# A two-layer diffusion step on one core: splits of 16 weight units on VectorE, the scan's work ahead of the q and k units, x to memory from SyncE, and later statistics

## The chip, the cores and the metric

The kernel runs on one NeuronCore of a Trainium2 chip. The time is the device time of one execution in microseconds, measured on the chip; three executions of the kernel before took 1505.66 to 1508.61 us, with a median of 1507.27.

## What is computed

Two layers of a hybrid backbone act on 640 tokens (128 of a prompt, 512 latent ones) with 1024 features, all in fp32. Every sub-layer is a norm, a modulation with shift and scale, a mixer, and a gated addition to x:

```python
hs = modulate(rmsnorm(xs, norm1_g[layer]), shift, scale)
if layer % 2 == 0:                       # pooling | gated convolution
    ys = even_mixer(hs, ab_w_in, pool_w, pool_scale, conv_w, ab_w_out)
else:                                    # attention | S5
    q_s, k_s, v_s, u_s = jnp.split(hs @ cd_w_in, 4, axis=-1)
    o_s = from_heads(neighbourhood_attention(to_heads(q_s), to_heads(k_s), to_heads(v_s), ...))
    d_s, _, _ = s5_bidirectional(u_s, state_s5_re, state_s5_im, *ssm_args)
    ys = jnp.concatenate([o_s, d_s], axis=-1) @ cd_w_out
xs = xs + gate1 * ys
hs = modulate(rmsnorm(xs, norm2_g[layer]), shift2, scale2)
xs = xs + gate2 * (jnp.square(jax.nn.relu(hs @ mlp_w1)) @ mlp_w2)
```

The prompt goes through the same layers, with plain attention instead of the windowed one. `s5_bidirectional` projects u to complex states, runs a linear recurrence over time in both directions, projects back, and multiplies with a gate (GLU).

## The kernel before

Features lie on the partitions: x is 8 row blocks of 128 features by 640 tokens. An fp32 product is made of three fp32r matmuls: a weight is split into wh (rounded) and wl (the rest), an activation into hh and hl (or dh and dl), and wl·hh, wh·hh and wh·hl are summed in PSUM.

Weights stream as 178 units of 512 KB, in the order of use: 0 to 15 and 16 to 23 the mixer of layer 0, 24 to 87 its MLP, 88 to 91 u of layer 1, 92 and 93 q0 and k0, 94 to 97 v, 98 to 103 q and k of the pairs of heads 1 to 3, 104 and 105 the GLU, 106 to 113 the output projection, 114 to 177 the second MLP. Of each unit SyncE's queue (SP) loads `raw`, ScalarE (ACT) rounds it to wh (L263), and wl is the difference, made by GpSimd (POOL, L270) or, for the units in the set ON_VECTOR, by VectorE (DVE, L268). The VectorE ones are put off: `defer` keeps them in a list until `flush`, which runs ahead of an evacuation, when TensorE comes to that unit, or when its buffer is needed again. At most four units are split at a time; `retire` frees one and splits the next.

Each engine has one queue, and works through it in the order in which the program is written; buffers and data are guarded by semaphores. The places that matter:

- A norm lies between the last four blocks of x (`out_units`, by halves of 320 tokens) and the first two units of the next layer (`in_units`). While TensorE makes the second half, VectorE does for each block the gated addition to x (L446), ACT its square (L388), and GpSimd, the last time VectorE, adds up the squares (acc, L389). Between them stand the modulated rows of the first half: t (VectorE, L431), hh (ACT, L434), hl (VectorE, L440). In `in_units` TensorE goes through k = 0 to 7 with two units at a time, first on half 0 (p = 0 and 1). `stats_half(1)` is written after the row k = 4 of p = 0: matmuls of acc (L395), a division, a square root on ACT (L399) and four small steps on VectorE (L398 to L403); `spread` (L412) after the first row of p = 1 lays the result over the partitions, and the rows of half 1 follow.
- Such a point comes three times in the part that the change touches: ahead of the MLP of layer 0 (units 24 on), ahead of u of layer 1 (units 88 on), and ahead of the second MLP (units 114 on).
- Ahead of u of layer 1, four DMAs on ACT's queue bring x to memory (`xst`, L1084), since its two buffers are used again (tags xa and xb: q and k, and the outputs of attention).
- At the end of the first MLP GpSimd also makes tables for S5 (`s5_build`, bd, s5f, s5g, L963 to L983) which TensorE transposes (L996).
- The S5 input (`s5_in`, blocks b = 0 to 15 with their tables et(b), L1228) is interleaved with the rows of the units of q0 and k0: `mid` lists pairs of row and block.
- The scan over S (`s5_scan`) runs on VectorE: first local sums (`add`, L1254 to L1257), then steps of width one, then copies, then eight fix-ups q = 0 to 7 (L1288, L1290). It is a generator; `scan_pump(n)` issues the next n pieces.
- Attention has 20 steps (`attention`, `step`) of softmax (L1386, L1388), exponentials on ACT, transposes and products; they stand behind the units of q and k by the table ATT (2, 3, 2, 3, 2, 3), the rest at the end. Within the steps a piece of the scan is pumped, `s5_turn` transposes S (copies L1472), and `s5_out(f)` (L1489, L1491) stands behind the steps of S5_OUT.

Of the kernel before, what the change touches and what calls it, by code (L numbers as in the profile page):

```python
# [7 lines left out]
F32R = mybir.dt.float32r  # L8
# [5 lines left out]
T = 640  # L14
TP = 128
EPS = 1e-6
KC = 8
# [158 lines left out]

ON_VECTOR = {*range(16, 24), *range(40, 80), *range(104, 106)}

N_EARLY = 88

# [1 line left out]

ATT = (2, 3, 2, 3, 2, 3)

S5_OUT = (9, 16, 18, 19)


class Rows:  # L190
# [12 lines left out]
class Net:  # L203
# [289 lines left out]
    def in_units(self, u0, rhs, evac, nxt, ahead=True):  # L493
        for h in range(2):
            for p in range(2):
                pt = self.ps()
                us = (u0 + 2 * p, u0 + 2 * p + 1)
                for k in range(KC):
                    for i, u in enumerate(us):
                        self.mms([(pt[:, i, :320], HALVES[h])], u, rhs[k], 128 * k, k == 0, k == KC - 1)  # L500
                    if h == 0 and p == 0 and k == 4:
                        self.stats_half(1)
                    if h == 0 and p == 1 and k == 0:
                        self.spread()
                        nxt(1, range(KC))
                self.flush()
                evac(h, p, pt)
                if h == 1:
                    for u in us:
                        self.retire(u, p == 0 or ahead)  # L510
# [551 lines left out]
    def layer1(self, u0, nxt_in, nxt_out):  # L1062
        nc, one, tc, A = self.nc, self.one, self.tc, self.A
# [12 lines left out]
        uf = one.tile([128, 4, 8, 80], F32, name="uf", tag="va")  # L1076
# [3 lines left out]
        self.scr = [dl[:, a:a + 640] for a in (3712, 4352)]  # L1080
        self.S = one.tile([128, 32, 2, 90], F32, name="S", tag="dh")
        self.load()
        for f in range(0, KC, 2):
            nc.scalar.dma_start(self.xst[:, f:f + 2], self.x.pair(f))  # L1084
        self.in_units(u0, self.hs, lambda h, p, pt: self.u_out(uf, h, p, pt), nxt_in, False)

        xq = one.tile([128, 4, T], F32, name="xq", tag="xa")
        self.q, self.k = (xq[:, 0], xq[:, 2]), (xq[:, 1], xq[:, 3])
        o = one.tile([128, 4, T], F32R, name="o0", tag="xb")
        self.os = [(o[:, 0], o[:, 1]), (o[:, 2], o[:, 3])]  # L1090
        att = self.attention()
        next(att)

        def qk(j, s, mid=()):
            u = u0 + 4 + 2 * j + s + (4 if j else 0)
            pt = self.ps()
            for k in range(KC):
                for b in (b for a, b in mid if a == k):
                    self.s5_in(b)
                self.mms(self.both(pt), u, self.hs[k], 128 * k, k == 0, k == KC - 1)  # L1100
            self.flush()
            o = (self.q, self.k)[s][j % 2]
            nc.scalar.activation(o.rearrange("p (a b) -> p a b", a=2), pt[:, :, :320], AF.Copy, scale=0.125 if s == 0 else 1.0)
            self.bias_ahead()
            self.turn(u)
            if s:
                nc.sync.dma_start(A["nk"][:, j], o[:, 0:128])

        qk(0, 0, [(4 + b, b) for b in range(4)])
        qk(0, 1, [(2 * (b - 4) // 3, b) for b in range(4, 16)])  # L1110
        self.scan = self.s5_scan()
        self.at = [one.tile([128, 8, 128], F32, name="at0"), None]
        nc.sync.dma_start(self.at[0], self.ast[:, 0:8])
        o = one.tile([128, 2, T], F32R, name="o1")
        self.os.append((o[:, 0], o[:, 1]))
        self.v_units(u0 + 6)
        self.step_no, self.yf = 0, None

        def step():
            next(att)  # L1120
            i = self.step_no
            self.step_no += 1
            self.scan_pump(1)
            if 8 <= i < 12:
                self.s5_turn(2 * i - 16)
                self.s5_turn(2 * i - 15)
            if i in S5_OUT:
                self.s5_out(S5_OUT.index(i))

        next(att)  # L1130
        for j in range(1, 4):
            for s in range(2):
                qk(j, s)
                for _ in range(ATT[2 * j - 2 + s]):
                    step()
            if j == 1:
                for q in range(2):
                    self.ft_load(q)
        o = one.tile([128, 2, T], F32R, name="o2", tag="la")
# [98 lines left out]
    def s5_scan(self):  # L1238

        S, v = self.S, self.nc.vector
        Z = S.rearrange("p n m c -> p (n m) c")
        sh = lambda w: [128, 32, 2, w]
        c = self.carry.rearrange("p (i n m k) -> p i n m k", i=2, n=32, m=2)
        rows = lambda i: c[:, i].rearrange("p n m k -> p (n m) k")
        v.memset(S[:, :, :, 0:10], 0.0)
        v.tensor_copy(S[:, :, 0, 2], self.s5sc[:, 3])
        v.tensor_scalar(S[:, :, 1, 2], self.s5sc[:, 4], -1.0, None, op0=OP.mult)
        yield  # L1250

        def add(cur, prv, j, w):
            t1, t2 = (t[:, :64 * w].rearrange("p (n m k) -> p n m k", n=32, m=2) for t in self.scr)
            v.tensor_mul(t1, self.apr[:, :, :, j:j + 1].to_broadcast(sh(w)), prv)  # L1254
            v.tensor_mul(t2, self.api[:, :, :, j:j + 1].to_broadcast(sh(w)), prv[:, :, ::-1])
            v.tensor_add(cur, cur, t1)
            v.tensor_add(cur, cur, t2)  # L1257

        add(S[:, :, :, 12:13], S[:, :, :, 2:3], 0, 1)
        yield  # L1260
        for j in range(1, 8):
            add(S[:, :, :, 10 * j + 10:10 * j + 20], S[:, :, :, 10 * j:10 * j + 10], 0, 10)
            yield

        add(S[:, :, :, 81:84:2], S[:, :, :, 80:83:2], 7, 2)
        f = self.one.tile([128, 2, 32], F32, name="fin")
        v.tensor_copy(f[:, 0], S[:, :, 0, 81])
        v.tensor_scalar(f[:, 1], S[:, :, 1, 81], -1.0, None, op0=OP.mult)
        self.nc.sync.dma_start(self.A["st"], f)
        yield  # L1270
        for k in range(4, 9):
            add(S[:, :, :, 80 + k:81 + k], S[:, :, :, 79 + k:80 + k], 7, 1)
            yield

        v.tensor_copy(Z[:, :, 1], Z[:, :, 80])
        v.tensor_copy(Z[:, :, 3:10], Z[:, :, 82:89])
        v.tensor_copy(rows(0), Z[:, :, 1:10])
        v.memset(rows(0)[:, :, 1:2], 0.0)
        v.tensor_copy(c[:, 1], c[:, 0, :, ::-1])
        yield  # L1280
        w = [128, 8, 7, 9]
        for q in range(8):
            n = slice(8 * q, 8 * q + 8)
            cur = Z[:, n, 10:80].rearrange("p a (j k) -> p a j k", k=10)[:, :, :, 1:10]
            ts = [t[:, :504].rearrange("p (a j k) -> p a j k", a=8, j=7) for t in self.scr]
            for i, (t, a) in enumerate(zip(ts, (self.apr, self.api))):
                a = a.rearrange("p n m j -> p (n m) j")[:, n, 0:7]
                v.tensor_mul(t, a[:, :, :, None].to_broadcast(w), rows(i)[:, n][:, :, None].to_broadcast(w))  # L1288
            for t in ts:
                v.tensor_add(cur, cur, t)  # L1290
            if q % 2:
                yield

    def v_units(self, u0):
        nc = self.nc
# [285 lines left out]
```

## Time and profile before

| | us |
|---|---|
| median of 3 runs | 1507.27 |
| the profiled execution | 1508.45 |
| its span | 1506.4 |
| TensorE busy | 1441.6 |
| VectorE busy | 883.3 |
| GpSimd busy | 623.8 |
| ACT busy | 483.9 |

The mean granted clock of TensorE over the span was 0.976 of full speed. A timeline row gives the start in us from the span's start, the duration, the engine, the line, what is written from what, and, in brackets, for how long the engine was idle before and what ended that. TensorE is busy nearly throughout; the short idle stretches and the stretches at a lower clock are what remains. A wait is read in two steps: which instruction of TensorE waits, and what its releaser in turn was waiting for.

### The profile page before, as it was taken

The numbers are of one execution on the slowest core, as the hardware profiler recorded it, in microseconds if no ns is written. First come the engines' busy times: TensorE is split into PE (matmuls) and PEld (weight loads), VectorE is DVE, ScalarE is ACT, GpSimd is POOL, SyncE is SP. The second block draws the span as 40 slices with busy tenths as digits, with TensorE's granted clock in tenths as the row PEclk, the third lists the DMA queues.
The fourth block names the chain that finished last, engine by engine and source line by source line (L and its number), as shares of the span: only waits on it lengthen the run. The fifth ranks groups of instructions, "written<-read, shape, count | busy, mean of one in ns | idle before, by whom it ended". The sixth has DMA issues, their size and how long they took to land.

```text
span 1506.4 us, 24126 instructions
## 1 busy us (share of the span) xinstructions
PE 1441.6 (96%) x9757; PEld 1409.8 (94%) x9757; DVE 883.3 (59%) x1602; ACT 483.9 (32%) x856; POOL 623.8 (41%) x445
## 2 busy tenths in 40 slices
PE   7999999999999999899899979999999999999997
PEld 7999899999999999899888878999999999999997
DVE  7899975899898888824429575336561221221223
ACT  4321234313323422333332435534421321321321
POOL 2333032327797778645324312053333333333342
PEclk9999999999999999999889979999999999999999
DMA  9245531514554445434762312621342222222211
GB/s 378 83 169 180 185 125 57 170 57 168 194 173 164 174 164 174 140 96 138 260 195 91 97 49 95 219 84 56 119 148 70 82 72 70 84 72 70 84 57 70
DMA packets 73966, 193.30 MB, mean 128 GB/s; under 512 B 15360, under 2 KB 23936, under 8 KB 73344
## 3 DMA queue, kind: packets, MB, share of 16 engines
q1 hardware_dynamic: 68400, 186.37, 36.5%
q10 hardware_dynamic: 5456, 5.40, 1.1%
q8 instruction: 77, 1.26, 0.4%
q14 instruction: 33, 0.27, 0.1%
HBM read 170.51 MB, written 22.54 MB: 128 GB/s over the span
## 4 chain that ended last, share of the span: by engine, by line
PE 70%; DVE 14%; issue 6%; POOL 3%; ACT 3%; DMA 2%; ACTq 0%; DVEq 0%; SPq 0%; POOLq 0%
PE pp L301 62%; DVE condb L332 3%; DVE hl L440 1%; PE bk L1424 1%; PE pp L1491 1%; PE pp L1306 1%; POOL wl L270 1%; PE bk L1228 1%; DVE x L446 1%; DMA raw<-wts 1%; ACT wh L263 1%; POOL s5q L964 1%; PE pp L1406 1%; DVE wl L268 1%; PE bk L996 1%
## 5 line engine op out<-in xcount | busy, mean ns | idle before, releaser
L270 POOL TENSOR_TENSOR wl<-raw,wh 128x1024 fp32r<-128x1024 f32 x128 | 316.4, 2476 | 617.9 <-ACT wh L263 613.9
L301 PE MATMUL pp<-hh,wl 128*128 128x320 f32 x1472 | 363.4, 318 | 2.3 <-POOL wl L270 1.2
L301 PE MATMUL pp<-hl,wh 128*128 128x320 f32 x1472 | 356.9, 313 | 7.1 <-DVE hl L440 5.1
L301 PE MATMUL pp<-hh,wh 128*128 128x320 f32 x1472 | 356.5, 313 | 0.0
L263 ACT ACTIVATE wh<-raw 128x1024 fp32r<-128x1024 f32 x178 | 186.2, 1051 | 321.1 <-PE pp L301 228.8
L301 PE MATMUL pp<-dh,wl 128*128 128x320 f32 x1152 | 280.1, 310 | 5.5 <-DVE x L446 2.7
L301 PE MATMUL pp<-dl,wh 128*128 128x320 f32 x1152 | 277.9, 309 | 0.0
L301 PE MATMUL pp<-dh,wh 128*128 128x320 f32 x1152 | 277.9, 309 | 0.0
L301 PEld LDWEIGHTS pp<-hl,wh 128*128 128x128 f32 x1472 | 254.6, 191 | 9.2 <-DVE hl L440 6.3
L301 PEld LDWEIGHTS pp<-hh,wl 128*128 128x128 f32 x1472 | 254.7, 192 | 5.5 <-issue 2.6
L301 PEld LDWEIGHTS pp<-hh,wh 128*128 128x128 f32 x1472 | 255.6, 192 | 0.0
L446 DVE SCALAR_TENSOR_TENSOR x<-pp,mod,x 128x128 f32<-128x128 f32 (+2 forms) x240 | 91.4, 432 | 242.7 <-PE pp L301 242.4
L301 PEld LDWEIGHTS pp<-dh,wl 128*128 128x128 f32 x1152 | 195.9, 188 | 8.8 <-issue 5.5
L301 PEld LDWEIGHTS pp<-dl,wh 128*128 128x128 f32 x1152 | 196.5, 188 | 0.3 <-DVE dl L451 0.3
L301 PEld LDWEIGHTS pp<-dh,wh 128*128 128x128 f32 x1152 | 196.5, 188 | 0.0
L332 DVE SCALAR_TENSOR_TENSOR condb<-ada,condb 128x1024 bf16<-128x1024 f32 x124 | 184.6, 1489 | 2.3
L772 DVE SCALAR_TENSOR_TENSOR pp<-pp,t 128x640 f32<-128x640 f32 x64 | 53.1, 830 | 190.2 <-ACT t L771 190.2
L771 ACT ACTIVATE t<-pp 128x640 f32<-128x640 f32 x64 | 45.1, 704 | 259.0 <-PE pp L301 243.2
L389 POOL TENSOR_TENSOR acc<-acc,sq 128x320 f32<-128x320 f32 (+1 forms) x36 | 40.0, 1112 | 117.1 <-ACT sq L388 112.5
L268 DVE TENSOR_TENSOR wl<-raw,wh 128x1024 fp32r<-128x1024 f32 x50 | 69.3, 1387 | 0.0
L388 ACT ACTIVATE sq<-x 128x320 f32<-128x320 f32 (+1 forms) x51 | 29.0, 570 | 117.2 <-DVE x L446 110.9
L774 DVE TENSOR_TENSOR dl<-pp,dh 128x640 fp32r<-128x640 f32 x64 | 52.6, 821 | 3.6
(249 smaller groups left out, 1633.2 us busy)
## 6 DMA issues: line engine op xcount, KB each, us to landing
raw<-wts SPq DMA_DIRECT2D x178, 512.0 KB, 3.5
ada<-ada SPq DMA_DIRECT2D x80, 512.0 KB, 4.5
spare<-ada SPq DMA_DIRECT2D x16, 512.0 KB, 3.6
est<-s5e SPq DMA_DIRECT2D x16, 256.0 KB, 5.0
fst<-s5fc SPq DMA_DIRECT2D x16, 256.0 KB, 2.0
et<-est SPq DMA_DIRECT2D x16, 256.0 KB, 3.7
ft<-fst SPq DMA_DIRECT2D x8, 512.0 KB, 4.1
x<-x SPq DMA_DIRECT2D x8, 320.0 KB, 5.4
```

The source lines that it names most:

```text
L263: self.nc.scalar.activation(wh, raw, AF.Copy)
L268: self.defer(lambda: self.nc.vector.tensor_sub(wl, raw, wh.bitcast(F32)))
L270: self.nc.gpsimd.tensor_sub(wl, raw, wh.bitcast(F32))
L301: self.nc.tensor.matmul(o, a[:, w], b[:, s], start=first and n == 0, stop=last and n == 2)
L332: self.nc.vector.scalar_tensor_tensor(self.junk, a, 1.0, self.condb[:, c], op0=OP.mult, op1=OP.mult, accum_out=self.mod[:, l, j, f, c:c + 1])
L388: self.nc.scalar.activation(q, self.x[f][:, s], AF.Square)
L389: (self.nc.vector if f >= last else self.nc.gpsimd).tensor_add(self.acc[:, s], self.acc[:, s], q)
L440: self.nc.vector.scalar_tensor_tensor(o, t, b, h.bitcast(F32), op0=OP.add, op1=OP.subtract)
L446: self.nc.vector.scalar_tensor_tensor(self.x[f][:, s], p[:, s.start - 320 * h:s.stop - 320 * h], self.mod[:, l, j, f, c:c + 1], self.x[f][ ...
L771: self.nc.scalar.activation(t, p, AF.Relu)
L772: self.nc.vector.scalar_tensor_tensor(p, p, 0.0, t, op0=OP.max, op1=OP.mult)
L774: self.defer(lambda: self.nc.vector.tensor_sub(dl, p, dh.bitcast(F32)))
```

## The change

- ON_VECTOR gets 16 units more: 24 to 27, 80 to 83, 88 to 91 and 114 to 117. VectorE makes their wl, GpSimd no longer.
- `stats_half(1)` is written two rows later, after k = 6.
- The four DMAs of x to memory leave ACT's queue. SP issues two after the evacuation of half 0, p = 1, and two after the unit of k0. The tile o0, which uses the second buffer of x again, is made after the units of v.
- The blocks of the S5 input stand one row later with q0 (5, 6, 7, 7) and two to a row from row 1 on with k0.
- The scan is no longer pumped in the steps but ahead of the six units of q and k, in portions of ATT_SCAN; a fix-up is a piece of its own. S is turned after the steps 6, 9, 11 and 13, and the first part of the S5 output stands behind step 8.

```diff
-ON_VECTOR = {*range(16, 24), *range(40, 80), *range(104, 106)}
+ON_VECTOR = {*range(16, 28), *range(40, 84), *range(88, 92), *range(104, 106), *range(114, 118)}
-S5_OUT = (9, 16, 18, 19)
+S5_OUT = (8, 16, 18, 19)
+
+S5_TURN = (6, 9, 11, 13)
+ATT_SCAN = (5, 3, 2, 2, 2, 1)
...
-                    if h == 0 and p == 0 and k == 4:
+                    if h == 0 and p == 0 and k == 6:
                         self.stats_half(1)
...
-        for f in range(0, KC, 2):
-            nc.scalar.dma_start(self.xst[:, f:f + 2], self.x.pair(f))
-        self.in_units(u0, self.hs, lambda h, p, pt: self.u_out(uf, h, p, pt), nxt_in, False)
+
+        def keep_x(f):
+            for f in (f, f + 2):
+                nc.sync.dma_start(self.xst[:, f:f + 2], self.x.pair(f))
+
+        def evac(h, p, pt):
+            self.u_out(uf, h, p, pt)
+            if h == 0 and p == 1:
+                keep_x(0)
+
+        self.in_units(u0, self.hs, evac, nxt_in, False)
...
-        qk(0, 0, [(4 + b, b) for b in range(4)])
-        qk(0, 1, [(2 * (b - 4) // 3, b) for b in range(4, 16)])
+        qk(0, 0, [(min(5 + b, 7), b) for b in range(4)])
+        qk(0, 1, [(1 + (b - 4) // 2, b) for b in range(4, 16)])
+        keep_x(4)
...
-            self.scan_pump(1)
-            if 8 <= i < 12:
-                self.s5_turn(2 * i - 16)
-                self.s5_turn(2 * i - 15)
+            if i in S5_TURN:
+                f = S5_TURN.index(i)
+                self.s5_turn(2 * f)
+                self.s5_turn(2 * f + 1)
...
             for s in range(2):
+                self.scan_pump(ATT_SCAN[2 * j - 2 + s])
                 qk(j, s)
...
-            if q % 2:
-                yield
+            yield
```

On VectorE, in the last round of the second norm (ahead of u of layer 1), before:

```order
L440 SCALAR_TENSOR_TENSOR hl<-t,mod,hh 128x192
L446 SCALAR_TENSOR_TENSOR x<-pp,mod,x 128x320
L389 TENSOR_TENSOR acc<-acc,sq 128x320
L431 SCALAR_TENSOR_TENSOR t<-x,gs,bk 128x128
L431 SCALAR_TENSOR_TENSOR t<-x,gs,bk 128x192
```

and after the change (the lines have moved by three):

```order
L443 SCALAR_TENSOR_TENSOR hl<-t,mod,hh 128x192
L271 TENSOR_TENSOR wl<-raw,wh 128x1024
L449 SCALAR_TENSOR_TENSOR x<-pp,mod,x 128x320
L392 TENSOR_TENSOR acc<-acc,sq 128x320
L434 SCALAR_TENSOR_TENSOR t<-x,gs,bk 128x128
```

A split stands between the low parts of one round and the x of the next; the same holds for the rounds before it and for the other two norms. The fourth split stands behind the last hl here, and behind the steps of the statistics in the first and the third norm.

On SP, from u of layer 1 to the unit of k0 (up is u in the scan's layout, uds its copy in memory, rpb a bias table, et the tables of S5), before:

```order
L1212 DMA et<-est 128x512 x4
L252 DMA raw<-wts 128x1024
L1206 DMA up<-uds 128x8x80 x2
L252 DMA raw<-wts 128x1024 x2
L1206 DMA up<-uds 128x8x80 x2
L252 DMA raw<-wts 128x1024
L1331 DMA attc<-rpb 64x1x265 x4
L1212 DMA et<-est 128x512 x4
```

and after:

```order
L1226 DMA et<-est 128x512 x4
L255 DMA raw<-wts 128x1024
L1089 DMA xst<-x 128x1280 x2
L1220 DMA up<-uds 128x8x80 x2
L255 DMA raw<-wts 128x1024 x2
L1220 DMA up<-uds 128x8x80 x2
L255 DMA raw<-wts 128x1024
L1344 DMA attc<-rpb 64x1x265 x4
L1226 DMA et<-est 128x512 x4
```

Two of the four transfers of x now stand ahead of the first loads of up; the other two stand further on, behind the unit of k0.

On VectorE in attention, where the second pair of fix-ups is done (L1288 and L1290 are one fix-up, L1472 the copies of the turn, L1386 and L1388 the softmax), before:

```order
L451 TENSOR_TENSOR o_7555<-pp,o_7555 128x128
L1288 TENSOR_TENSOR up<-apr,up 128x504
L1288 TENSOR_TENSOR up<-api,up 128x504
L1290 TENSOR_TENSOR S<-S,up 128x8x7x9 x2
L1288 TENSOR_TENSOR up<-apr,up 128x504
L1288 TENSOR_TENSOR up<-api,up 128x504
L1290 TENSOR_TENSOR S<-S,up 128x8x7x9 x2
L1472 COPY S<-tn 64x8x80 x2
L1386 TENSOR_TENSOR pp<-pp,bm 128x2x256
L1388 TENSOR_REDUCE sm<-pp 128x2
```

and after, ahead of the unit of k in which they are now issued, with the end of the step before it:

```order
L454 TENSOR_TENSOR o_8031<-pp,o_8031 128x128
L1485 COPY S<-tn 64x8x80 x2
L1302 TENSOR_TENSOR up<-apr,up 128x504
L1302 TENSOR_TENSOR up<-api,up 128x504
L1304 TENSOR_TENSOR S<-S,up 128x8x7x9 x2
L1302 TENSOR_TENSOR up<-apr,up 128x504
L1302 TENSOR_TENSOR up<-api,up 128x504
L1304 TENSOR_TENSOR S<-S,up 128x8x7x9 x2
L271 TENSOR_TENSOR wl<-raw,wh 128x1024
L1401 TENSOR_REDUCE sm<-pp 128x2
```

Before, the next step's softmax follows two fix-ups and the copies; now two fix-ups stand once in front of a whole unit, and a split of the GLU's weights after them.

## Rows read from the trace of the kernel before

**Rows 1.** Stretches: length, busy us (count) by engine, granted clock, DMA share, GB/s.
```profile
208.00:240.00 32.00, 29.10 (x181) 28.55 (x180) 23.46 (x55) 14.29 (x31) 12.18 (x7) 0.89 0.21 66
605.00:640.00 35.00, 30.13 (x202) 28.81 (x200) 29.90 (x41) 13.22 (x26) 25.62 (x25) 0.95 0.41 138
699.00:737.00 38.00, 31.77 (x178) 30.57 (x178) 28.48 (x61) 16.14 (x37) 18.99 (x13) 0.82 0.55 187
752.00:790.00 38.00, 34.34 (x230) 33.88 (x229) 8.87 (x32) 11.94 (x22) 11.68 (x8) 0.87 0.67 199
819.00:937.00 118.00, 105.74 (x758) 98.43 (x755) 75.28 (x159) 55.55 (x153) 34.70 (x34) 0.91 0.29 87
1022.00:1050.00 28.00, 25.11 (x154) 24.57 (x154) 20.63 (x49) 12.85 (x28) 12.17 (x7) 0.88 0.23 75
```

**Rows 2.** Waits of TensorE in the first norm: total us, times, longest.
```profile
PE pp L301 <- DVE hl L440: 1.6, 1, 1.6
PE bk L395 <- DVE acc L389: 1.3, 1, 1.3
```

**Rows 3.** Waits of TensorE from the second norm to k0.
```profile
PE bk L412 <- DVE st L403: 3.1, 1, 3.1
PE bk L1228 <- ACT S L1233: 2.0, 1, 2.0
```

**Rows 4.** Waits of TensorE in the last units of the first MLP.
```profile
PE bk L996 <- POOL s5f L965: 4.9, 2, 3.6
```

**Rows 5.** Waits of TensorE in attention.
```profile
PE pp L1432 <- DVE o L451: 5.8, 2, 4.4
PE pp L1491 <- DVE S L1472: 3.3, 1, 3.3
```

**Rows 6.** Timeline of VectorE in the second norm: start, duration, instruction, idle before.
```profile
705.79 0.54 DVE L446 SCALAR_TENSOR_TENSOR x<-pp,mod,x 128x320 f32<-128x320 f32 x1
706.25 1.24 DVE L431 SCALAR_TENSOR_TENSOR t<-x,gs,bk 128x128 f32<-128x128 f32 x4
708.16 3.22 DVE L440 SCALAR_TENSOR_TENSOR hl<-t,mod,hh 128x128 fp32r<-128x128 f32 x4 [0.67 <-ACT hh L434]
711.31 0.54 DVE L446 SCALAR_TENSOR_TENSOR x<-pp,mod,x 128x320 f32<-128x320 f32 x1
```

**Rows 7.** Timeline of GpSimd in the same round.
```profile
707.92 2.40 POOL L270 TENSOR_TENSOR wl<-raw,wh 128x1024 fp32r<-128x1024 f32 x1
```

**Rows 8.** Timeline of VectorE in attention.
```profile
888.22 0.68 DVE L1288 TENSOR_TENSOR up<-api,up 128x504 f32<-128x504 f32 x1
888.81 1.40 DVE L1290 TENSOR_TENSOR S<-S,up 128x504 f32<-128x504 f32 x2
...
899.27 1.23 DVE L268 TENSOR_TENSOR wl<-raw,wh 128x1024 fp32r<-128x1024 f32 x1
```

**Rows 9.** Timeline of TensorE at full clock, pairs of matmuls in k0's unit.
```profile
753.71 0.46 PE L301 MATMUL pp<-hh,wh 128*128 128x320 f32 x2
754.01 0.45 PE L301 MATMUL pp<-hl,wh 128*128 128x320 f32 x2
```

**Rows 10.** Timeline of GpSimd at the end of the first MLP.
```profile
625.80 2.46 POOL L270 TENSOR_TENSOR wl<-raw,wh 128x1024 fp32r<-128x1024 f32 x1 [8.69 <-ACT wh L263]
...
631.20 0.79 POOL L965 TENSOR_TENSOR s5f<-s5f,s5q 128x288 f32<-128x288 f32 x1
...
634.37 1.65 POOL L965 TENSOR_TENSOR s5f<-s5f,s5q 128x288 f32<-128x288 f32 x1
```

**Rows 11.** Timeline of ACT and its queue behind the second norm.
```profile
720.00 8.06 ACTq L1084 DMA_DIRECT2D xst<-x  x3
728.12 0.21 ACT L399 ACTIVATE st<-st 128x3 f32<-128x3 f32 x1 [7.97 <-DMA ast<-a]
```

**Rows 12.** Timeline of VectorE in the scan's local sums.
```profile
819.40 0.82 DVE L1256 TENSOR_TENSOR S<-S,up 128x640 f32<-128x640 f32 x1
820.25 2.92 DVE L1257 TENSOR_TENSOR S<-S,up 128x640 f32<-128x640 f32 x1
```

More of the change, by code (lines that the diff above doesn't have):

```diff
@@ L1082, in layer1 @@
         self.load()
-        for f in range(0, KC, 2):
-            nc.scalar.dma_start(self.xst[:, f:f + 2], self.x.pair(f))
-        self.in_units(u0, self.hs, lambda h, p, pt: self.u_out(uf, h, p, pt), nxt_in, False)
+        def keep_x(f):
[6 more added lines that the diff above has]
+        self.in_units(u0, self.hs, evac, nxt_in, False)
         xq = one.tile([128, 4, T], F32, name="xq", tag="xa")
         self.q, self.k = (xq[:, 0], xq[:, 2]), (xq[:, 1], xq[:, 3])
-        o = one.tile([128, 4, T], F32R, name="o0", tag="xb")
-        self.os = [(o[:, 0], o[:, 1]), (o[:, 2], o[:, 3])]
+        self.os = []
         att = self.attention()
@@ L1116, in layer1 @@
         self.v_units(u0 + 6)
+        o0 = one.tile([128, 4, T], F32R, name="o0", tag="xb")
+        self.os = [(o0[:, 0], o0[:, 1]), (o0[:, 2], o0[:, 3])] + self.os
         self.step_no, self.yf = 0, None
```

## Prediction

> **What bounds the kernel now.** I read the stretches that the change touches first, for TensorE's busy time and granted clock; then the waits inside each; then the timelines of the engine that a wait names. In six stretches, 289 us in all, TensorE is busy for 256 us [rows 1]: it is the bound there, so a change that neither adds nor removes a matmul can win only what TensorE idles or runs at its lower clock. Idle time is length minus PE busy: 2.9 us (first norm), 4.9 (the last MLP units of layer 0), 6.2 (second norm), 3.7 (the unit of k0 with the S5 input), 12.3 (attention), 2.9 (third norm), together 32.9. The clock column is a mean of 1.2 and 2.4 GHz; a stretch of length L, clock c and busy share b loses about L x (1 - c) x b: 3.2, 1.5, 5.7, 4.5, 9.5 and 3.0, together 27.4. So some 60 us can be had at most.
>
> The waits say who is late. In the first norm TensorE waits 1.6 us for hl and 1.3 us for the sum of squares, both from VectorE [rows 2]; the third loses the same 2.9. In the second it also waits 3.1 us for the statistics, and of the 3.7 us at k0, 2.0 are put down to the eviction into S [rows 3]. In the units 80 to 83 all 4.9 us go to GpSimd's s5f [rows 4]. In attention 5.8 us are for o and 3.3 for S, both from VectorE [rows 5].
>
> **The change part by part.** *First and third norm.* In the last rows of an output unit VectorE goes round x, t, hl, x, and the next matmuls are fed from it. One round takes 711.31 - 705.79 = 5.5 us [rows 6]. Its four hl take 3.2 us, while four t of the same shapes take 1.24; GpSimd's wl, 2.4 us, runs at just that time [rows 7]. Moved to VectorE, a wl costs 1.23 us where nothing competes [rows 8]. The new round is .5 (x) + 1.2 (t) + .7 (waiting for hh) + 1.25 (hl) + 1.2 (wl), about 4.8, or 4.6 with its overlaps: .7 to .9 shorter, some 2.4 over three rounds. That ends the wait of 1.6 for hl at row 4. The wait of 1.3 for the sum of squares ends since the statistics are asked for two rows later; a row is six matmuls, three pairs at .295 (754.01 - 753.71), .88 us [rows 9]. What is late next is row 6: its hh and hl come from the last round, behind sq, wh and the sum; counting on from the shifted x, hh is 1.2 and hl another .7 behind. And the fourth moved split (unit 27, 117) stands behind the statistics on VectorE when TensorE wants it for the next pair of units: one wl, 1.2. Of 2.9 + 3.2 = 6.1 lost in the stretch, 3.1 come back as waits: 3.0 are won if the clock stays up, 1.5 if these waits cost half of the clock's old price. I take 2.3 each, 4.6 for both. Ends: 4.7 each if only 1.4 of the new waits show and no clock falls; -.2 each if all new waits are there and the clock falls as before.
>
> *Units 80 to 83.* GpSimd was done with its earlier rows at 617.1, then its queue waited 8.7 us for ACT's wh to make a wl, with bd and s5f queued behind that [rows 10]. With the four splits on VectorE, which makes those of units 40 to 79 in the same mix of work already, bd and s5f can start in that gap. They take from the end of wl, 628.3, to 636.0; started by 621 they are done by 629, at least 7 us earlier, against 4.9 that TensorE waited. Of 4.9 + 1.5 I take all, 6.4. Lower end 3.0: one step of s5f took 1.65 us where another took .79 [rows 10], and at that price for all of its steps about half of the wait stays.
>
> *Second norm, x to memory, S5 input.* ACT issues four transfers of x from 719.6 to 728.1, and the square root of the statistics stands behind them with 7.97 us of idle time [rows 11] (the row puts it down to another transfer; what keeps ACT is its own queue of issues). TensorE waits 3.1 us for this. SP takes two of these transfers after the second pair of units and two after k0. ACT is then free at 720.1. TensorE lost 6.2 idle and, to the spread, about half of the clock's 5.7: 9.1; I charge 1.9 back for row 6. The other half, 2.8, follows the wait that goes: 10.0 so far. Next comes S5's input: block b needs et(b), and SP issues et(4) behind weights, up<-uds and bias loads. That chain starts from the same spread and moves ahead with it, less what x costs on SP; the blocks stand one row (.88) later. So its 3.7 of waits and 4.5 of clock largely stay: I take 1.0 of 8.2. Sum 11. Ends: 7 (two issues at ACT's price, 8.06 / 3 = 2.7 each, less the row and the slack before et) and 15 (half of the 8.2 goes too).
>
> *Attention.* Fix-ups, turning copies and softmax stand in one row on VectorE. Before, a step could carry two fix-ups; one is two products at .68 and two sums, 1.40 together, 2.7 us [rows 8], so 5.4 in front of the next softmax: the waits for o and S. After, this work stands ahead of the six q and k units, of 48 matmuls or 24 x .295 = 7.1 us each [rows 9]: two fix-ups (5.4) and at some a wl (1.2), 6.6, so VectorE keeps up by half a microsecond. S is turned two steps ahead of the matmuls on it rather than one, so 3.3 goes. Of 12.3 + 9.5 = 21.8 lost, the waits that are neither o nor S, 3.2, stay; I charge as much again for moments in which VectorE is a little late, and .4 of clock: 15. Ends: 9 (each of six units leaves 1 us of wait and as much in clock) and 17.5 (little beside the 3.2 stays).
>
> Sum: 4.6 + 6.4 + 11 + 15 = 37.0. The profiled execution took 1508.45 us, 2.05 over its span and 1.18 over the median. 1508.45 - 37.0 = 1471.4, on the scale of the median 1470. With all upper ends (9.4 + 6.4 + 15 + 17.5 = 48.3) it is 1459; with all lower ends (-.4 + 3 + 7 + 9 = 18.6) 1489.
>
> **The rivals.** *A, the cost only changes place.* If VectorE and GpSimd block each other whatever stands where, moving wl wins nothing: the norms give 0 instead of 4.6, the units 80 to 83 give 3.0, the second norm loses the shorter rounds (3 of 11): 3 + 8 + 15 = 26, 1481. For it: hl at 3.2 beside GpSimd's wl [rows 6, 7], s5f at 1.65 [rows 10]. Against it: wl is half as long on VectorE, 1.23 against 2.4. The Trainium skill, Perfetto Trace Analysis, section "Optimizing Scalar/DVE Operations", states this rival as a rule: the two share a read port, "so offloading operations between those two might not help". The slow hl beside wl agrees with a shared port; that moving is useless does not follow from these rows.
>
> *B, VectorE becomes late.* With 16 x 1.2 = 19 us more it stays last in the norms (0 of 4.6, 7 of 11), and three of the six units in attention leave 1.25 us of wait and as much in clock, so 15 become 7.5: 6.4 + 7 + 7.5 = 21, 1486. For it: VectorE is named in most waits. Against it: each round of a norm has 2 us of blocked hl to give.
>
> *C, SP holds up what follows.* The x transfers stand ahead of up<-uds, weights and et; 2.7 each make S5's input 5 us later, with clock, so 11 become 4: 1477. For it: the 8.06 us for three issues [rows 11]. Against it: before, the queue was as full from the same transfers.
>
> *D, slower.* Ahead of q and k, the fix-ups run at the price that a row of the scan shows at its worst: a sum at 2.92 us [rows 12] where the one before it took .82, 3.5 times as much. At that price two fix-ups take 19, 12 over the unit's 7.1. The four units with two of them then lose 48 us and some 12 in clock, against 21.8 lost in attention before: 38 worse there, 22 better elsewhere, 1523. It decides from about 2.7 times the price on (two fix-ups at 14.6, 7.5 over, 30 + 12 against 21.8 + 22). Against it: such rows stand alone among fast ones, and the fix-ups of before ran at .68 [rows 8].
>
> *E, no change.* The waits only move: row 6 and unit 27 wait for the same VectorE chain, S5's input for the same SP chain, and the softmax for the same fix-ups one unit later: 1507. Against it: the ACT issues and GpSimd's queue are real detours that vanish.
>
> **How the numbers follow.** The forecast has .64, A .08, B .12, C .05, D .06, E .05. Predicted: 1470. To hold 8 in 10 the range takes in the bounds of the forecast, and with them A, B and C: 1459 to 1489; D, E and the tails are left out. About 0.2% (3 us) is what a measurement of this kernel can tell from no change. Faster: .64 + .08 + .12 + .05 = .89; same .05; slower .06.
>
> **What would show it.** In the profile after: hl x4 near 1.3 us in the norms and a round under 5; the square root of the second norm right behind hh; no wait for s5f; some 3 us of waits left in S5's input; in attention no wait over 1.5 us for o, none for S, and its clock at .97 or more. The norms are wrong if hl still takes 3 us, or if unit 27's wl is waited for over 2 us; the second norm if up<-uds is issued later after the spread than before; attention if a fix-up's product takes over 1 us, or softmax rows wait behind fix-ups for over 3 us. The total comes out too low above all if the clock falls again at each of the small waits.

## The result

The changed kernel takes 1487.78 us, the median of 19 executions (1479.98 to 1510.62), against 1507.86 us for the kernel before. The ratio is 0.9855, with a 95% interval of 0.9842 to 0.9867, or 20 to 24 us less. Five of the 19 executions ran at a lower clock and took 1506 to 1511 us; the ratios, here and below, leave out what lies over 1.5% above a kernel's fastest execution and the medians do not, so kernels are compared by their ratios. The forecast was 1470 with a range of 1459 to 1489: the time lies at the slow end of the range, and of 37 us that were expected some 22 came.

The profiled execution of the changed kernel took 1483.03 us, with a span of 1481.3, 25.1 less than the span before. The first view of it is the six stretches between the same matmuls as in [rows 1] (the columns are those of [rows 1]):

```profile
208.00:239.20 31.20, 29.32 (x181) 28.40 (x180) 22.01 (x60) 14.29 (x31) 2.65 (x3) 0.89 0.21 68
604.30:632.60 28.30, 28.30 (x201) 27.50 (x200) 24.27 (x34) 12.26 (x23) 26.72 (x27) 1.00 0.49 171
691.60:723.00 31.40, 28.92 (x178) 28.42 (x178) 23.89 (x61) 14.87 (x35) 7.57 (x8) 0.89 0.39 121
738.00:775.70 37.70, 32.68 (x230) 31.93 (x229) 9.44 (x33) 11.91 (x22) 11.60 (x8) 0.91 0.75 231
804.80:914.00 109.20, 101.13 (x758) 93.80 (x756) 76.97 (x158) 56.15 (x153) 33.79 (x34) 0.97 0.31 94
998.90:1024.50 25.60, 22.50 (x154) 21.70 (x153) 19.24 (x54) 13.70 (x29) 2.63 (x3) 1.00 0.20 62
```

TensorE has the same 9757 matmuls in both traces, so the start of the same matmul in each tells how much was won up to there. The table sets the terms of the forecast beside these differences, stretch by stretch:

| stretch | forecast | won in the trace |
|---|---|---|
| first norm | 2.3 | 0.8 |
| units 80 to 83 | 6.4 | 6.7 |
| second norm | 10.0 | 6.7 |
| k0 with S5's input | 1.0 | 0.1 |
| attention | 15 | 8.8 |
| third norm | 2.3 | 2.3 |
| all, with the rest | 37.0 | 25.3 |

This execution is some 3 us faster than its kind (1486 is 0.9855 of the kernel before), so each row may be off by a fall of the clock, which cost 1.7 or 3.4 us each time in these stretches of its trace. The row of S5's input scatters most: in three further traces with the same code and the same transfers in this stretch (the kernels below with the statistics at k = 4, with later turns and with hh first) it lost 0.0, 3.5 and 5.0 us where this trace won 0.1.

The waits of TensorE in the changed kernel, in the first norm:

```profile
PE pp L304 <- ACT hh L437: 1.9, 1, 1.9
```

from the second norm to k0:

```profile
PE bk L1242 <- ACT S L1247: 4.4, 1, 4.4
PE pp L304 <- ACT hh L437: 2.5, 1, 2.5
PE bk L1242 <- DMA up<-uds: 0.7, 1, 0.7
```

in attention (o is its output, sm the sums of the softmax):

```profile
PE pp L1445 <- DVE o L454: 4.0, 2, 3.3
PE pp L1445 <- DVE sm L1413: 2.1, 1, 2.1
```

and in the third norm:

```profile
PE pp L304 <- ACT hh L437: 1.9, 1, 1.9
PE pp L304 <- DVE wl L271: 1.1, 1, 1.1
```

Gone are the waits of [rows 2], those of [rows 4] (in the stretch of the units 80 to 83 TensorE no longer waits for anything, and its busy time equals the length), the one for the statistics of [rows 3], and the one for S of [rows 5]. New are those for hh and for wl; S5's input and o are still waited for.

A round of VectorE in the first norm, which answers to [rows 6], in the timeline:

```profile
217.46 0.55 DVE L449 SCALAR_TENSOR_TENSOR x<-pp,mod,x 128x320 f32<-128x320 f32 x1
217.92 1.25 DVE L434 SCALAR_TENSOR_TENSOR t<-x,gs,bk 128x128 f32<-128x128 f32 x4
219.85 1.41 DVE L443 SCALAR_TENSOR_TENSOR hl<-t,mod,hh 128x128 fp32r<-128x128 f32 x4 [0.68 <-ACT hh L437]
221.17 1.22 DVE L271 TENSOR_TENSOR wl<-raw,wh 128x1024 fp32r<-128x1024 f32 x1
222.30 0.54 DVE L449 SCALAR_TENSOR_TENSOR x<-pp,mod,x 128x320 f32<-128x320 f32 x1
```

The four hl take 1.41 us where they took 3.22, the split 1.22, and the round 222.30 - 217.46 = 4.84 us in place of 5.5. GpSimd at the end of the first MLP, as in [rows 10]:

```profile
616.35 2.47 POOL L986 COPY bd<-bc 64x32 f32<-64x32 f32 x2
...
624.40 1.67 POOL L968 TENSOR_TENSOR s5f<-s5f,s5q 128x288 f32<-128x288 f32 x1
```

It goes from s5g to bd without a wait, and s5f is done at 626.1; before it was done at 636.0. ACT in the second norm, as in [rows 11]:

```profile
714.82 0.21 ACT L402 ACTIVATE st<-st 128x3 f32<-128x3 f32 x1 [2.94 <-DVE st L401]
```

The square root waits for VectorE's first step now and not for ACT's own queue.

### The profile page after: what moved, and what is told of

The parts are those of the page before. It is cut to its first block, busy times and chain, and to the rows that moved or that the text cites. A ratio compares the mean times of both kernels' runs of the same rounds, so it can differ in the third digit from the quotient of the medians.

```text
span 1481.3 us, 24120 instructions
## 1 busy us (share of the span) xinstructions
PE 1428.6 (96%) x9757; PEld 1397.0 (94%) x9757; DVE 882.5 (60%) x1618; ACT 484.7 (33%) x856; POOL 587.8 (40%) x429
## 4 chain that ended last, share of the span: by engine, by line
PE 73%; DVE 13%; issue 5%; ACT 3%; POOL 2%; DMA 2%; SPq 0%; ACTq 0%; DVEq 0%; POOLq 0%
PE pp L304 64%; DVE condb L335 3%; PE bk L1437 2%; DVE wl L271 1%; PE pp L1319 1%; DVE x L449 1%; PE pp L1504 1%; PE bk L1242 1%; DVE hl L443 1%; PE pp L1419 1%; ACT wh L266 1%; PE pp L1391 1%; DMA raw<-wts 1%; PE bk L999 1%; DVE pb L681 1%
## 5 line engine op out<-in xcount | busy, mean ns | idle before, releaser
L273 POOL TENSOR_TENSOR wl<-raw,wh 128x1024 fp32r<-128x1024 f32 x112 | 277.3, 2480 | 605.2 <-ACT wh L266 545.0
L304 PEld LDWEIGHTS pp<-hh,wl 128*128 128x128 f32 x1472 | 251.9, 190 | 14.1 <-ACT hh L437 7.0
L271 DVE TENSOR_TENSOR wl<-raw,wh 128x1024 fp32r<-128x1024 f32 x66 | 90.0, 1363 | 0.0
```

Of the source, the lines that this page charges most:

```text
L271: self.defer(lambda: self.nc.vector.tensor_sub(wl, raw, wh.bitcast(F32)))
L273: self.nc.gpsimd.tensor_sub(wl, raw, wh.bitcast(F32))
L304: self.nc.tensor.matmul(o, a[:, w], b[:, s], start=first and n == 0, stop=last and n == 2)
```

## Which part gave what

Theory: each part works by the mechanism that the forecast named. Rivals: GpSimd and VectorE only exchange a cost (A), VectorE becomes late in attention (B), the transfers of x cost the S5 input what they gave ACT (C). Four kernels carry one part each. A fifth part, the blocks of the S5 input one row later, was not run alone.

**The 16 splits alone.**

```diff
-ON_VECTOR = {*range(16, 24), *range(40, 80), *range(104, 106)}
+ON_VECTOR = {*range(16, 28), *range(40, 84), *range(88, 92), *range(104, 106), *range(114, 118)}
```

> The kernel before with one line of the change alone: the 16 units more in ON_VECTOR. Theory (moving a split takes GpSimd off VectorE's back in the norms, and off its own queue ahead of s5f): no wait for s5f, 6.4 us; in each of the three norms the wait for hl goes and the wait for the sum of squares shrinks, some 2 us each: 12 us faster, 1496, hl x4 near 1.3 us. Rival A (the cost only changes place): hl still near 3 us, the norms as before, at most 3 us from units 80 to 83: 1505.

Measured: 1495.18 us, ratio 0.9906 (0.9882 to 0.9931), about 14 us less. In the first norm, VectorE's timeline, and then what TensorE waits for:

```profile
222.47 1.41 DVE L440 SCALAR_TENSOR_TENSOR hl<-t,mod,hh 128x128 fp32r<-128x128 f32 x4 [0.68 <-ACT hh L434]
223.79 1.22 DVE L268 TENSOR_TENSOR wl<-raw,wh 128x1024 fp32r<-128x1024 f32 x1
```

```profile
PE bk L395 <- DVE acc L389: 1.7, 1, 1.7
PE pp L301 <- DVE wl L268: 0.6, 1, 0.6
```

Rival A falls: hl is down to 1.41 us with no other edit, the wait for it is gone, and so is the one for s5f; the units 80 to 83 win the same 6.7 us as in the whole. What remains is the wait for the sum of squares (1.7) and a little for the fourth split (0.6).

**The scan's part alone.** ATT_SCAN, S5_TURN, S5_OUT[0] and the piece per fix-up, on the kernel before.

```diff
+S5_TURN = (6, 9, 11, 13)
+ATT_SCAN = (5, 3, 2, 2, 2, 1)
...
+                self.scan_pump(ATT_SCAN[2 * j - 2 + s])
                 qk(j, s)
```

> The kernel before with the scan's part alone (ATT_SCAN, S5_TURN, S5_OUT, a fix-up as a piece of its own). The forecast's term, 15 us, would give 1493. What the trace after shows in attention, 8.6 us, would give 1499. Rival B (VectorE late at the k units) says the same 7.5 to 9 and waits for o of 2 us and more at the end of a unit.

Measured: 1496.96 us, ratio 0.9925 (0.9903 to 0.9948), about 11 us less. The trace puts 10.3 us of this into attention, and shows the waits of the changed kernel:

```profile
PE pp L1435 <- DVE o L454: 3.1, 2, 2.5
PE pp L1435 <- DVE sm L1403: 2.1, 1, 2.1
```

So the waits for o and for the softmax belong to this part and not to the additional splits.

**x to memory on SP alone.**

```diff
-        for f in range(0, KC, 2):
-            nc.scalar.dma_start(self.xst[:, f:f + 2], self.x.pair(f))
...
+            if h == 0 and p == 1:
+                keep_x(0)
...
+        keep_x(4)
```

> The kernel before with the four transfers of x on SP alone, as in the change (two behind the second pair of units, two behind k0, o0 made after v). Theory: the square root no longer waits for ACT's queue, 3.1 us of waiting and about 3 us of clock go: 1502. Rival C (SP holds up weights, up and et): the 6 us come back in S5's input: 1507, with waits there over 5 us instead of 3.7.

Measured: 1506.14 us, ratio 0.9988 (0.9974 to 1.0002): at most 4 us, and no change at all lies within the interval. TensorE's waits in S5's input:

```profile
PE bk L1237 <- ACT S L1242: 3.9, 1, 3.9
PE bk L1237 <- DMA up<-uds: 2.8, 1, 2.8
PE bk L1237 <- DMA et<-est: 1.4, 1, 1.4
```

The second norm wins 6.0 us in the trace, as expected; but the waits in S5's input rise from 3.7 to 8.0 us, and that stretch loses 2.2. Rival C is right in kind. Here the blocks of the S5 input stand at their old rows; in the changed kernel, with the blocks one row later, the waits are 5.0. Whether the later rows took off these 3 us is not shown.

**The later statistics alone.**

```diff
-                    if h == 0 and p == 0 and k == 4:
+                    if h == 0 and p == 0 and k == 6:
```

> The kernel before with the statistics two rows later alone (k = 6 instead of 4). Theory: the wait for the sum of squares (1.3 us) goes, the one for hl at row 4 (1.6) stays, and row 6 waits for the last round of VectorE, which is not earlier: about the same time, 1507, within 2 us. If the rows' place alone were the gain: 4 to 8 us faster, 1501.

Measured: 1508.84 us, ratio 1.0000 (0.9988 to 1.0012). TensorE in the first norm:

```profile
PE pp L301 <- DVE hl L440: 3.3, 2, 1.7
PE pp L301 <- ACT hh L434: 1.5, 1, 1.5
```

The wait for the sum (1.3) is replaced by one for hh (1.5) and a second one for hl (1.7) at row 6. Asking later for the sum doesn't help a chain that hangs on the same last round.

The four ratios taken one by one come to 14 + 11 + 2 + 0 = 27 us, the whole gives 22. The five intervals together leave about 6 us either way, so this difference of 5 is not shown by itself; the following kernels test what may cost something in the combination.

## What is lost in the combination

**Statistics back at k = 4, all else as changed.**

```diff
-                    if h == 0 and p == 0 and k == 6:
+                    if h == 0 and p == 0 and k == 4:
```

> The changed kernel with the statistics back at row k = 4. Theory (VectorE's last round sets the end of the norm, not the place of the statistics): a wait of 1.7 to 2.3 us for the sum of squares takes the place of the 1.9 to 2.5 us for hh at row 6, the time stays within 1.5 us of the changed kernel, 1486. The forecast (the later row takes off the wait for the sum): 3 to 4 us slower, 1490.

Measured: 1482.87 us, ratio 0.9812 (0.9791 to 0.9834), which doesn't overlap with the changed kernel's 0.9842 to 0.9867. So with the splits on VectorE the later place of the statistics costs: 1 to 11 us by the ends of the intervals, some 6 by their middles. I had expected no difference. In the first norm, and likewise in the third, TensorE waits

```profile
PE bk L398 <- DVE acc L392: 1.7, 1, 1.7
```

in place of 1.9 for hh, and in the third norm the wait for the fourth split shrinks from 1.1 to 0.6. With the clock the trace wins 2.1 and 1.1 us more in these two norms than the changed kernel. The other traces agree: over the first norm the two kernels with the splits and k = 4 (this one and the splits alone) win 2.9 and 3.6 us on the kernel before, and over the third 3.4 each; the changed kernel, the three with x moved or left out, the one with later turns and the last one below, all with k = 6, win 0.8 to 1.9 and 1.7 to 2.3. That is about half of the difference; the rest is not located, since this profiled execution took 1484.08 us and others of the same kernel 1476.5 and 1477.0.

**hh ahead of wh on ACT**, since row 6 waits for hh, which stands behind wh.

```diff
                 if h == 1:
-                    self.turn(u0 + f)
                     nxt(0, (range(0), range(2, 4), range(4, 6), range(6, 8))[i])
+                    self.turn(u0 + f)
```

> The changed kernel, with hh of a round ahead of wh on ACT (the modulation is written before the next unit's split). Theory: row 6 waits 1.9 to 2.5 us in each norm since hh stands behind wh (1.04 us) there; VectorE's round also loses the .7 us in which it waits for hh: a round of 4.1 to 4.2 us in place of 4.84, the row 6 wait gone or under .5: 1.5 to 2.5 us for each of three norms, 1480, and less of the lower clock. Rival: PE then waits for the later wh and wl (units 26, 27) by as much: 1486.

Measured: 1486.75 us, ratio 0.9850 (0.9834 to 0.9866): the same as the changed kernel. Two x of VectorE's timeline in the first norm, and then TensorE's waits there:

```profile
219.83 0.55 DVE L449 SCALAR_TENSOR_TENSOR x<-pp,mod,x 128x320 f32<-128x320 f32 x1
...
224.35 0.54 DVE L449 SCALAR_TENSOR_TENSOR x<-pp,mod,x 128x320 f32<-128x320 f32 x1
```

```profile
PE pp L304 <- ACT hh L437: 1.2, 1, 1.2
PE pp L304 <- DVE wl L271: 1.1, 1, 1.1
```

The round falls only to 4.5 us, for VectorE now waits 0.24 us for wh. In the first norm the wait for hh falls from 1.9 to 1.2 and one of 1.1 for the fourth split is new, as the rival said; my expectation missed that the split itself needs wh. In the second and the third norm the waits fall by 0.6 and 0.7 and none is new. The unchanged time doesn't settle what this is worth: over the three norms this trace wins 3.5 us more than the changed kernel's, most of it in the first, where its clock didn't fall (1.00 against 0.89), and S5's input, which this edit doesn't touch, loses 5.1 more.

**The transfers of x, later, priced, and earlier.** Three kernels tell what x costs S5's input. In the changed kernel two transfers go out on SP at 730, and the DMA view of 725 to 760 has them, with the median time from issue to landing at the end of the row:

```profile
xst<-x SPq DMA_DIRECT2D x2, 640.0 KB, 9.0
```

On ACT's queue before, it was 4.4 us. The first pieces of u's way through memory, on ACT's and on SP's queue:

```profile
732.40 0.34 ACTq L1216 DMA_DIRECT2D uds<-uf  x1
...
739.38 1.65 SPq L1220 DMA_DIRECT2D up<-uds  x2
```

u goes back out 7.0 us after it was sent to memory; before, it was 2.2 (746.46 to 748.69). In all five traces with the transfers at this place it is 7.0 to 7.9. First, issue them later:

```diff
-            if h == 0 and p == 1:
+            if h == 1 and p == 1:
                 keep_x(0)
```

> The changed kernel, with the first two transfers of x issued on SP after the second half's evacuation (h = 1, p = 1) rather than the first's: they then stand behind all of u's way through memory and the weights of q0. Theory (the transfers of x share the DMA engines with u's way to memory, so up<-uds is issued 7 us late and S5's input waits): up<-uds goes out 3 to 5 us earlier, the 5.0 us of waits in S5's input fall to 3 or less, and the time by 2 to 4 us with the clock: 1483 against 1486. Rival (S5's input waits for the queue of weights, whatever x does): same time and waits, within 1.5 us.

Measured: 1488.17 us, ratio 0.9875 (0.9860 to 0.9890), not better. The wait for S falls to 0.5 us, but

```profile
PE bk L1242 <- DMA et<-est: 7.2, 1, 7.2
```

is new. u goes back out after 3.6 us, as I expected, but the transfers, issued at 748.11, now lie beside the loads of the tables (issued from 753.86 on), which take 5.2 to 5.8 us to land in place of 4.5 to 4.7; more than what the wait for S lost comes back in the wait for them. My theory named the wrong neighbour, u's way to memory alone. Second, the price:

```diff
-            if h == 0 and p == 1:
-                keep_x(0)
...
-        keep_x(4)
+        keep_x(0, 4)
+        keep_x(4, 4)
```

Here keep_x(f, g) writes the blocks from f on out of x's blocks from g on, so this kernel doesn't keep the first half of x; it only prices the two transfers.

> The changed kernel without the store of x's first half ahead of q0: its place in memory is written from the second half, behind k0, so the part of x kept there is another and the traffic in front of S5's input is gone. This prices those two transfers. Theory: waits in S5's input 1 to 2 us in place of 5.0, up<-uds issued 2 to 4 us after uds as in the kernel before: 3 to 6 us faster than the changed kernel, 1481. Rival: same time, S5's input is held by the load of the weights of k0 alone.

Measured: 1482.58 us, ratio 0.9834 (0.9818 to 0.9851): by the middles about 3 us less than the changed kernel, though the intervals overlap a little, with

```profile
PE bk L1241 <- ACT S L1246: 2.2, 1, 2.2
PE bk L1241 <- DMA et<-est: 0.7, 1, 0.7
```

in place of 5.0 us (I had expected 1 to 2). So the two transfers cost 2 us of waiting and some 3 us of time. The wait for S that is left hangs on weights: ACT makes S right behind the rounding of a unit (wh) that waited 2.0 us for its load. ACT's timeline:

```profile
749.89 1.06 ACT L266 ACTIVATE wh<-raw 128x1024 fp32r<-128x1024 f32 x1 [2.00 <-DMA raw<-wts]
```

Third, a place that costs nothing. The first four blocks of x are final before the last four are made, and the DMA engines have little to do from 685 to 705 (a share of 0.19):

```diff
         if nxt is None:
             return
+        self.pre()
         for h in range(2):
...
-            if h == 0 and p == 1:
-                keep_x(0)
```

where `pre` issues the two transfers once, ahead of the last four blocks of the first MLP.

> The changed kernel, with the first two transfers of x issued on SP ahead of the last four blocks of the first MLP, where the first four blocks of x are final and the DMA engines are idle for some 20 us (685 to 705). Theory (those transfers cost S5's input 2 to 3 us, since they lie beside u's way through memory): the same gain as without them, waits in S5's input near 3 us in place of 5, 1482.5. Rival (only leaving them out helps, since SP's queue or the weights then stand behind them at the earlier place): 1486 or slower.

Measured: 1483.69 us, ratio 0.9836 (0.9821 to 0.9850), and in S5's input

```profile
PE bk L1240 <- ACT S L1245: 2.2, 1, 2.2
PE bk L1240 <- ACT wh L266: 0.4, 1, 0.4
```

The price is won back in full, with nothing left out. The stretch of S5's input says the same as the ratios: it wins 2.4, 2.7 and 3.2 us in the three traces without these transfers beside it (this one, the one before it and the last kernel below), and 0.1 at most in the four with them. Last, x on ACT's queue as before with all else as changed:

> The changed kernel with the four transfers of x back on ACT's queue ahead of u of layer 1, all else as changed. Theory from the traces: the wait for the statistics in the second norm is back with 3.1 us and its clock, waits in S5's input fall from 5.0 to some 3.2 us: 1488 to 1489. The forecast (ACT's queue cost 7 to 8 us with the clock, SP's next to nothing): 1493. Rival C in full (SP's way costs as much as ACT's): 1486.

Measured: 1490.32 us, ratio 0.9862 (0.9837 to 0.9887), the same as the changed kernel within the intervals, and by the ratio 1487, near what rival C said. Together with the kernel that carries this part alone: as placed in the change, moving x to SP is worth nothing that can be measured. In the trace of that part alone S5's input gives back 2.2 of the 6.0 us that the second norm wins; what takes the rest is not shown.

**The wait for o in attention.** The timeline of VectorE in the changed kernel, at the fifth of the six units, and then that of GpSimd:

```profile
877.85 0.49 DVE L1485 COPY S<-tn 64x640 f32<-64x640 f32 x1 [1.23 <-ACT tn L1484]
...
879.55 1.40 DVE L1304 TENSOR_TENSOR S<-S,up 128x504 f32<-128x504 f32 x2
...
882.05 3.56 DVE L1304 TENSOR_TENSOR S<-S,up 128x504 f32<-128x504 f32 x2
...
886.65 0.69 DVE L1399 TENSOR_TENSOR pp<-pp,bm 128x512 f32<-128x512 f32 x1
```

```profile
881.96 2.38 POOL L273 TENSOR_TENSOR wl<-raw,wh 128x1024 fp32r<-128x1024 f32 x1 [8.01 <-ACT wh L266]
```

The first pair of sums takes 1.40 us, the second 3.56, and the difference of 2.16 is nearly the length of GpSimd's split, which began 0.09 us ahead of it. That and a late start (the copies of a turn wait for tn, the piece of S that ACT has ready for them) make up the 3.3 us for o. In six other traces with these turns the sums are fast and VectorE's own split behind them meets GpSimd's (3.38 us in place of 1.22 in each); the softmax is as late, and the wait is 2.4 to 2.5. The test turns S one step later:

```diff
-S5_TURN = (6, 9, 11, 13)
+S5_TURN = (6, 10, 12, 14)
```

> The changed kernel, with the turns of S after the steps 6, 10, 12, 14 in place of 6, 9, 11, 13. Theory: at the fifth of the six units the two fix-ups stand behind a turn's copies that wait 4 us for ACT, so the last sum runs beside GpSimd's wl (3.56 us in place of 1.40) and o comes 3.34 us late; with the turn one step later they start 3 to 4 us earlier, end before that wl, and the wait goes: 3 us and 1.7 of clock, 1482. Rival (the fix-ups and the softmax are too much for the unit anyway): a wait for o of 2 us or more stays there, or comes at the next unit: 1486.

Measured: 1484.29 us in the median of four (1482.82 to 1502.86), ratio 0.9877 (0.9818 to 0.9936; the interval is too wide to rank it). The trace decides:

```profile
878.22 1.40 DVE L1304 TENSOR_TENSOR S<-S,up 128x504 f32<-128x504 f32 x2
...
880.72 1.39 DVE L1304 TENSOR_TENSOR S<-S,up 128x504 f32<-128x504 f32 x2
882.03 1.22 DVE L271 TENSOR_TENSOR wl<-raw,wh 128x1024 fp32r<-128x1024 f32 x1
```

Both pairs are done before GpSimd's split, which comes at 884.52 here, and the wait of 3.3 us at this unit is gone; one of 1.7 us comes at the next unit, where it was 0.6. Attention wins 11.3 us in place of 8.8, so about half of what I expected; the trace as a whole gains nothing, mainly since S5's input, which this edit doesn't touch, loses 3.5.

**Early x, later turns, and one piece of the scan moved to the second unit.**

```diff
-S5_TURN = (6, 9, 11, 13)
-ATT_SCAN = (5, 3, 2, 2, 2, 1)
+S5_TURN = (6, 10, 12, 14)
+ATT_SCAN = (4, 4, 2, 2, 2, 1)
...
```

> The same with early transfers of x, S turned after steps 6, 10, 12, 14, and one piece of the scan moved from the first of the six units to the second (4, 4, 2, 2, 2, 1). Theory: -3 us for x, -2 us for the turn, and the wait of 2.1 us for o in the first unit, where the scan's small sums stand ahead of the softmax, shrinks by the piece's 1.2 us: 1480. Rival (the gains share a stretch of lower clock and don't add, or the piece makes the second unit late): 1483.

Measured: 1478.86 us, ratio 0.9812 (0.9792 to 0.9831). It is faster than both kernels: 28 us less than before and some 6 less than the changed one, and the intervals don't overlap. In attention

```profile
PE bk L1435 <- ACT pT L1420: 2.7, 4, 1.6
PE pp L1443 <- DVE o L454: 2.4, 2, 1.7
```

the wait of 2.1 us for the softmax's reciprocal (sm) is gone, and so is the longest for o. Its trace wins 14.1 us in attention, near the 15 of the forecast, with a fall of the clock of 1.7 just behind. This kernel has the statistics at k = 6 still. With k = 4 it may be faster; that wasn't run.

## Why the forecast was too low

Its sign and its range held, the sum did not: 37.0 expected, 22 found. In the trace, which won 25.3, the missing 11.7 lie in attention (6.2), the second norm (3.3), the first norm (1.5) and S5's input (0.9); the units 80 to 83 gave 0.3 more. Of the signs of being wrong that I had named, one came outright: up<-uds goes out 4.8 us later, counted from the same matmul behind the second norm. In attention no product of a fix-up was slow (0.68), but a wait for o of 3.3 us stands where I had none over 1.5. Step by step:

- *Units 80 to 83*: 6.4 expected, 6.7 in every trace with the splits on VectorE. The queue was the reason; s5f at its slower price (1.67 in the changed kernel too) came early enough not to matter. The lower end wasn't needed.
- *First and third norm, the splits*: a round of 4.8 expected, 4.84 found; hl 1.25 expected, 1.41 found. The new waits were named with their sizes: hh 1.2 and hl another 0.7, found as 1.9 for hh alone; the fourth split 1.2, found as 1.1 in the third norm. The forecast of 4.6 for both stands against 3.2 in this trace.
- *The statistics* are the step that failed in these norms. I credited the later row with ending the wait of 1.3 us and booked the new waits to the splits. The two kernels on k show that the row gave nothing alone and cost time in the combination: without it the splits leave 1.7 + 0.6 us of waits in the third norm, with it 1.9 + 1.1. Asking later moves the wait from the sum to the rows ahead of it, which need the same last round.
- *Second norm*: 10.0 expected, 6.7 found. The wait for the statistics went, as I said. The row-6 wait was set at 1.9 and is 2.5, and I let the whole clock loss of the second half go; the clock fell once more after the new wait (0.89 over the stretch, 1.00 in the last MLP units), some 3 us.
- *S5's input*: 1.0 expected, 0.1 found, 5.0 us of waits where I had some 3. Rival C, at .05, was the better account of it. Its delay of 5 us is there (up<-uds goes out 7.0 us after uds in place of 2.2), but it cost some 3 us of time and not 7; and its mechanism is right in part: not the issue on SP, which took 1.43 us for two (SP then stood idle from 731.5 to 739.4, waiting for u's copy in memory), but the transfers in flight, 9.0 us to land in place of 4.4, make u late. The 6.8 found for this term with the norm's part lie just under its lower end of 7.
- *Attention*: 15 expected, 8.8 in the trace of the whole and 10.3 in that of the part alone. That VectorE keeps up by half a microsecond was the mis-sized term. Two fix-ups and a split take 6.2 us where they meet nothing (877.03 to 883.25 with the later turns) against 6.6 computed, but I left out two things: the copies of a turn ahead of them, which wait for ACT, and a split of GpSimd's beside one of the sums, 2.2 us. And the first of the six units has the scan's small sums in front of its softmax: the five pieces take 10.5 us (809.3 to 819.9), of which 2.43 are one product of 64 columns that takes .27 otherwise. I had only priced the units with fix-ups. The lower end of 9 was also a slip: 21.8 less six times 2 is 9.8.
- *Rival B* had 1486, which is the time that came by the ratio, and near terms: 7 for the second norm with S5's input (6.8 found), 7.5 for attention (8.8). The agreement is luck in part. Its cause was the 19 us of further splits on VectorE, but the first and the third norm were not left at 0 (3.2 found), the scan's part alone, without these splits, waits for o and sm too (3.1 and 2.1), and with later turns the longest wait for o goes. It was right that VectorE would be late in attention.
- *Rival A* fell. Moving the splits gave 14 us alone. The sums that met a split of GpSimd's lost about its length and no more: what VectorE pays is not a rate but the length of what it runs into, and that is why it helps to take the long instruction from GpSimd. The Trainium skill, Perfetto Trace Analysis, section "Optimizing Scalar/DVE Operations", has the rule that moving operations between the two might not help; here it did. The Trainium skill, SBUF — State Buffer, section "Who interferes with whom", says that a VectorE instruction with two inputs in SBUF contends with a GpSimd instruction that reads SBUF, and that the ports which the two share are an exclusive lock; the 2.16 us lost beside a split of 2.38 agree with that.
- *Rival D* rested on the same rows read as a rate. 2.92 against .82 is one meeting with one instruction of GpSimd's, not a price for every sum: of the 16 sums of fix-ups in the changed kernel's trace one is slow.
- *Rival E* did not happen for the whole, but two of the five parts, the statistics and x as placed, do what it says.

## What to carry to other kernels

When a late chain is fed from one engine's rounds, shorten the round; asking later for one of its results moves the wait to the next. Price a slow row by what it ran into (here GpSimd's 2.4 us split), and look for the instructions that can meet it in the new order; a row that was fast before may meet it after the change. A transfer moved off a queue still shares the DMA engines with what lies beside it (9.0 us to land in place of 4.4 here): look for a stretch in which they have little to do and the data is final, as 685 to 705 here.

## What I had not expected of the hardware

- Small instructions lose as much as large ones: a product of 64 columns took 2.43 us (815.00) beside a split of 2.39 that GpSimd began at 814.91, while the next instruction of the same size took .27 (VectorE's timeline, then GpSimd's):

```profile
815.00 2.43 DVE L1269 TENSOR_TENSOR up<-api,S 128x64 f32<-128x64 f32 x1
817.35 0.27 DVE L1270 TENSOR_TENSOR S<-S,up 128x64 f32<-128x64 f32 x1
```

```profile
814.91 2.39 POOL L273 TENSOR_TENSOR wl<-raw,wh 128x1024 fp32r<-128x1024 f32 x1 [1.19 <-ACT wh L266]
```

- Executions of the changed kernel spread more than those of the kernel before: those behind the ratio from 1480 to 1491 us, against 1505.6 to 1510.4. The profiled traces of equal stages differ by falls of the clock of 1.7 or 3.4 us that come in one and not in another (the third norm, the same code in both, ran at 1.00 in the changed kernel's trace and at 0.94 in that of the kernel with later transfers). One trace therefore doesn't settle a difference of 3 us in a stage.
